# SwiGLU columns of both token tiles transposed in one batch and split in one instruction each

## The chip, the cores and the metric

One Trainium2 chip, one core of it. The metric is device time in microseconds of one execution of the whole program, a median over runs; lower is better.

## The reference

Two decoder layers over 256 tokens of width 1024. In each layer three attention mixers read one normalised input, an output projection adds to x, and a SwiGLU feed-forward (FFN) with 2816 inner columns follows. The FFN is the part that matters here:

```python
for l in range(DEPTH):              # DEPTH = 2
    ...
    x = x + mix @ w_out[l]
    h2 = rms_norm(x, ffn_norm_g[l])
    x = x + (jax.nn.silu(h2 @ w_gate[l]) * (h2 @ w_up[l])) @ w_down[l]
```

## The kernel before

All arithmetic is float32 through TensorE's fp32r type. Each product is made of three matmuls: every operand is split into a high part `h` (rounded by a copy to fp32r) and a low part `lo` (operand minus `h`), and `mm3` (L570 and after) issues high x high (L577), high x low weight (L578) and low x high weight (L579). Weights are split the same way, 1024 columns at a time, by a copy on ScalarE (L245, `wh<-raw`) and a subtraction on VectorE (L500, `wl<-raw,wh`).

The 256 tokens are two tiles of 128 (t = 0, 1; NT = 2). The FFN's 2816 columns are eleven chunks `fc` of 256, handled in the blocks (0), (1), (2,3), (4), (5,6), (7), (8,9), (10). A block of one chunk runs `alone`: for each tile, gate and up projections of 256 columns each into one PSUM bank. A block of two runs `strassen`: seven products, from which VectorE combines the gate and up sums of the four (chunk, tile) pairs in the order (second chunk, t=1), (second, t=0), (first, t=0), (first, t=1). For each pair a `glu_thread` then does: Silu of the gate half (L1184, ScalarE), times the up half (L1187 or L1190, VectorE) into a tile `p` of 256 columns; two 128x128 transposes on TensorE into a fresh PSUM bank (L595); a copy of their 256 columns to the high half of `f4` (L245 ScalarE, `qk<-bank`; `f4` lives in the buffer `qk`); and a subtraction to its low half (L1199, VectorE). Then the event `fev[fc][t]` lets `down` multiply `f4` by w_down into four PSUM banks, tile by tile. The down projection of a block follows the gate and up projections of the next block (inside `strassen` it stands after the fifth product).

No engine's order is written by hand. At build time a planner (`Timeline`) runs all these generators as threads. Each operation has an engine, a planned cost and a rank; the planner emits next the one that can start first by its clocks, and among equals the one of lower rank. The threads of SwiGLU have rank 10, the main thread of matmuls 50, the weight splits 60 once enough are ahead (5 before). The engines then run their queues strictly in the emitted order, so an operation that is later on the chip than in the plan holds up all that stands behind it on its engine. A `get` takes a free buffer: `PP` has seven tiles `p`, `BANK` eight PSUM banks, `HL` four split weights.

Of the kernel before, what the change touches and what calls it, by code (L numbers as in the profile page):

```python
# [9 lines left out]
F32 = mybir.dt.float32  # L10
# [5 lines left out]
P = 128  # L16
# [3 lines left out]
NT = S // P  # L20
# [3 lines left out]
NFC = DFF // FC  # L24
# [158 lines left out]
def hybrid_block(  # L183
# [18 lines left out]
    nc = tc.nc  # L202
    depth = w_in.shape[0]
    x_in = x_in[0]
    out = out[0]
# [16 lines left out]
    def slots(n, shape, tag):  # L222
        return Slots([tile_(shape, tag=tag) for _ in range(n)])


    def A(n, emit, sbuf=False, ap=0, bank=None):
        return ("op", [("ACT", n / 1.2 + (94 if sbuf else 51) + 93 * ap, emit)], bank)

    def V(n, emit, fast=False, ap=0, bank=None):
        return ("op", [("DVE", n / (1.92 if fast else 0.96) + 66 + 61 * ap, emit)], bank)  # L230
# [5 lines left out]
    def T(ns, emit):  # L236
        return ("op", [("PE", ns, emit)])

    def copy_op(dst, src, n, sbuf=False, scale=None, bank=None):

        ap = 0 if scale is None else 1

        def on_act():
            if scale is None:
                nc.scalar.activation(dst, src, AF.Copy)  # L245
            else:
                nc.scalar.activation(dst, src, AF.Copy, scale=scale)

        def on_dve():
            if scale is None:  # L250
                nc.vector.tensor_copy(dst, src)
            else:
                nc.vector.tensor_scalar_mul(dst, src, scale)

        a = A(n, on_act, sbuf, ap)[1]
        d = V(n, on_dve, sbuf, ap)[1]
        return ("op", a + d, bank)

    tl = Timeline()
# [3 lines left out]
    BANK = Slots(banks)  # L263
# [25 lines left out]
    PP = slots(7, [P, 3 * P], "p")  # L289
# [35 lines left out]
    def toks(t):  # L325
        return slice(t * P, (t + 1) * P)
# [7 lines left out]
    def quarters(b):  # L334
        return b.rearrange("p (k q) -> p k q", q=P)
# [229 lines left out]
    def drop(t, *key):  # L565
        ahead[0] -= 1
        HL.put(units[key]["hl"], t)
# [24 lines left out]
    def transposes(pairs):  # L592
        def emit():
            for o, i in pairs:
                nc.tensor.transpose(o, i, ident)  # L595

        return T(109 * len(pairs), emit)
# [576 lines left out]
        done.done(e)  # L1174


    def glu_thread(t, bank, src, full, f4_of, done):

        yield ("wait", full)
        ppt = yield ("get", PP)  # L1180
        ff = ppt[:, 0:FC]
        gu = bank if bank is not None else src[2]
        yield A(
            FC, lambda: nc.scalar.activation(ff, gu[:, 0:FC], AF.Silu), bank is None, bank=bank  # L1184
        )
        if bank is not None:
            e = yield V(FC, lambda: nc.vector.tensor_mul(ff, gu[:, FC : 2 * FC], ff), bank=bank)  # L1187
            BANK.put(bank, e)
        else:
            e = yield V(FC, lambda: nc.vector.tensor_mul(ff, gu[:, FC : 2 * FC], ff))  # L1190
            src[0].put(src[1], e)
        bank2 = yield ("get", BANK)
        b2 = quarters(bank2)
        e = yield transposes([(b2[:, k, :], ff[:, k * P : (k + 1) * P]) for k in range(2)])
        PP.put(ppt, e)
        f4 = yield from f4_of()
        h, lo = f4[:, 0:2, toks(t)], f4[:, 2:4, toks(t)]
        yield copy_op(h, b2[:, 0:2, :], 256, bank=bank2)
        e = yield V(256, lambda: nc.vector.tensor_sub(lo, b2[:, 0:2, :], h.bitcast(F32)), bank=bank2)  # L1199
        BANK.put(bank2, e)  # L1200
        done.done(e)

    def strassen_thread(at, ev, glu):
# [180 lines left out]
    def main():  # L1384
        for l in range(depth):
# [90 lines left out]
            full = [[Event(), Event()] for t in range(NT)]  # L1476
# [11 lines left out]
            for us, t in (((0, 1), 0), ((0,), 1), ((2, 3), 0), ((1,), 1), ((2, 3), 1)):  # L1488
# [6 lines left out]
                for u, k, kt, hf in order:  # L1495
                    wt = yield from weight(l, "out", OUT_ORDER[u][0], k=k)
                    yield ("wait", mix[mixed[u]][t])
                    e = yield mm3(
                        bk[t][hf], cur["mT"], kt, toks(t), wt, k, slice(512 * hf, 512 * hf + 512),
                        u == 0 and k == 0, u == 3 and k == 1,  # L1500
                    )
# [15 lines left out]
            def f4_of(fc):  # L1517
                def get():
                    yield ("wait", kept["over"])
                    if not f4s:  # L1520
                        f4s.append(tile_([P, 4, 4, S], F32R, tag="qk", own=False))
                    return f4s[0][:, fc % 4]

                return get

            fev = [[Event() for t in range(NT)] for fc in range(NFC)]
            x_ready[:] = [[Event(), Event()] for t in range(NT)]
            bk = full = None

            def down(fcs, t):  # L1530
                for fc in fcs:
                    key = (l, "down", fc)
                    yield ("wait", fev[fc][t])
                    f4 = f4s[0][:, fc % 4]
                    order = [(k, hf) for k in range(2) for hf in range(2)]
                    if fc == NFC - 1:
                        order.sort(key=lambda v: v[1])
                    for k, hf in order:
                        wt = yield from weight(*key, k=k)
                        e = yield mm3(  # L1540
                            bk[t][hf], (f4[:, 0:2], f4[:, 2:4]), k, toks(t), wt, k,
                            slice(512 * hf, 512 * hf + 512),
                            fc == 0 and k == 0, fc == NFC - 1 and k == 1,
                        )
                        if fc == NFC - 1 and k == 1:
                            full[t][hf].done(e)
                    if t == NT - 1:
                        drop(e, *key)
# [22 lines left out]
            def alone(fc):  # L1571
                for t in range(NT):
                    bank = yield ("get", BANK)
                    for u in (0, 4):
                        if fc == 0:
                            yield ("wait", h2_ready[t][u // 4])
                        for k in range(4):
                            wt = yield from weight(l, "gu", fc, u, k=k)
                            e = yield mm3(
                                bank, hT, u + k, toks(t), wt, k, slice(0, 512),  # L1580
                                u + k == 0, u + k == KT - 1,
                            )
                        if t == NT - 1:
                            drop(e, l, "gu", fc, u)
                    gfull = Event()
                    gfull.done(e)
                    tl.spawn(glu_thread(t, bank, None, gfull, f4_of(fc), fev[fc][t]), 10)

            def strassen(i, j, between):
                at = {}  # L1590
                ev = {k: Event() for k in "P1 P2 Q3 Q4 Q5 P6 P7".split()}

                def glu(t, n, src, when):
                    now = Event()
                    now.done(when)
                    fc = (i, j)[n]
                    tl.spawn(glu_thread(t, None, src, now, f4_of(fc), fev[fc][t]), 10)

                tl.spawn(strassen_thread(at, ev, glu), 8)
                lo8, hi8 = [tuple(h[:, ks] for h in hT) for ks in (slice(0, 4), slice(4, 8))]  # L1600
                s3, s1, s2, n4 = [(s_ready[o], kept, o) for o in range(4)]
                steps = [
                    ("P1", (lo8, 0), (l, "gu", i, 0)),
                    ("P7", s3, (l, "T3", i)),
                    ("Q5", s1, (l, "T1", i)),
                    ("P6", s2, (l, "T2", i)),
                    ("Q3", n4, (l, "gu", j, 4)),
                    None,
                    ("P2", (hi8, 0), (l, "gu", i, 4)),
                    ("Q4", (hi8, 1), (l, "T4", i)),  # L1610
                ]
                for step in steps:
                    if step is None:
                        yield from between
                        continue
                    name, a, key = step
                    at[name] = yield ("get", BANK)
                    if len(a) == 3:
                        yield ("wait", a[0])
                        aT, tok = kept["S"][a[2]], slice(0, P)  # L1620
                    else:
                        aT, tok = a[0], toks(a[1])
                    for k in range(4):
                        wt = yield from weight(*key, k=k)
                        e = yield mm3(
                            at[name], aT, k, tok, wt, k, slice(0, 512), k == 0, k == 3
                        )
                    drop(e, *key)
                    ev[name].done(e)
# [81 lines left out]
```

## Time and profile before

| | |
|---|---|
| median of 3 runs | 653.18 us (652.63 to 653.49) |
| profiled execution | 651.67 us, of which the span of the profile is 649.9 us |
| TensorE, VectorE, ScalarE, GpSimd busy | 636.6, 563.5, 401.2, 85.8 us |
| weight loads of TensorE busy | 521.6 us |
| granted clock of TensorE | 0.999 of full speed over the span |
| FFN of the first layer, of the second | some 147 to 330 us, some 465 to 647 us |

Busy time counts an instruction from its first to its last cycle, and neighbours overlap. So the time that an instruction takes from its engine is read from the distance between starts, not from its length. A matmul of 512 columns shows 0.39 us but starts 0.227 us after the one before it.

### The profile page before, as it was taken

To read this page: it belongs to the slowest core of one execution; us is meant where nothing else is said; L and a number is where in the kernel's file an instruction comes from. 1 tells how busy PE (TensorE), PEld (TensorE's weight loads), DVE (VectorE), ACT (ScalarE), POOL (GpSimd) and SP (SyncE) were. 2 spreads that over 40 slices of the span, in tenths; PEclk is the share of its full clock that TensorE was granted. 3 is DMA by queue.
4 is the path that set the end of the run, shared out by engine and by line. 5 is a ranking of instruction groups with operands and counts; after the bars stand their busy time and mean duration, and the time that the engine had idled before them with its cause. 6 is when DMAs were issued, how large, how long until landed. Compare 5 with 4: busy or idle time off the path is not lost.

```text
span 649.9 us, 8878 instructions
## 1 busy us (share of the span) xinstructions
PE 636.6 (98%) x3180; PEld 521.6 (80%) x3180; DVE 563.5 (87%) x948; ACT 401.2 (62%) x728; POOL 85.8 (13%) x115
## 2 busy tenths in 40 slices
PE   9999999999999999999999999999999999999997
PEld 8877887787787888878888788888777778888886
DVE  5889999666999999999487999985599899999971
ACT  6567587647656656556456675893677385575650
POOL 2513420200000000170020334300100000000000
PEclk9999999999999999999999999999999999999999
DMA  8972533608549458419747045352475475472631
GB/s 250 318 228 73 187 134 128 195 1 266 186 142 290 154 193 258 130 65 307 229 131 233 26 145 181 130 179 82 127 262 176 149 258 186 149 249 64 200 124 66
DMA packets 73777, 111.29 MB, mean 171 GB/s; under 512 B 2658, under 2 KB 54660, under 8 KB 73732
## 3 DMA queue, kind: packets, MB, share of 16 engines
q1 hardware_dynamic: 73700, 110.71, 52.8%
q8 instruction: 25, 0.41, 0.3%
q14 instruction: 20, 0.16, 0.1%
q10 hardware_dynamic: 32, 0.01, 0.0%
HBM read 109.66 MB, written 1.05 MB: 170 GB/s over the span
## 4 chain that ended last, share of the span: by engine, by line
PE 71%; DVE 18%; DMA 5%; ACT 2%; issue 2%; SPq 1%; POOL 0%; DVEq 0%; POOLq 0%; ACTq 0%
PE bank L577 21%; PE bank L579 20%; PE bank L578 20%; DVE wl L500 8%; PE bank L595 5%; DMA raw<-in_w_up_dram 3%; PE bank L996 2%; PE bank L1046 1%; DMA raw<-in_w_in_dram 1%; DVE raw L509 1%; DMA w<-in_diff_lambda_dram 1%; DVE qr L509 1%; DVE mL L509 1%; ACT wh L245 1%; DVE w L1211 1%
## 5 line engine op out<-in xcount | busy, mean ns | idle before, releaser
L245 ACT ACTIVATE wh<-raw 128x1024 fp32r<-128x1024 f32 (+3 forms) x207 | 210.8, 1040 | 98.9 <-PE bank L579 35.2
L500 DVE TENSOR_TENSOR wl<-raw,wh 128x1024 fp32r<-128x1024 f32 (+4 forms) x209 | 249.8, 1204 | 17.5 <-ACT wh L245 17.2
L577 PE MATMUL bank<-wh,hH 128*128 128x512 f32 (+3 forms) x488 | 191.6, 393 | 0.3 <-ACT hH L245 0.3
L578 PE MATMUL bank<-wl,hH 128*128 128x512 f32 (+3 forms) x488 | 186.1, 381 | 1.0 <-DVE wl L500 0.4
L579 PE MATMUL bank<-wh,hL 128*128 128x512 f32 (+3 forms) x488 | 185.2, 379 | 0.5 <-DVE hL L627 0.5
L578 PEld LDWEIGHTS bank<-wl,hH 128*128 128x128 f32 x488 | 92.0, 188 | 19.9 <-DVE wl L500 6.2
L577 PEld LDWEIGHTS bank<-wh,hH 128*128 128x128 f32 x488 | 91.9, 188 | 18.6 <-issue 3.6
L579 PEld LDWEIGHTS bank<-wh,hL 128*128 128x128 f32 x488 | 91.7, 188 | 17.3 <-DVE hL L627 0.8
L577 PE MATMUL bank<-wh,qk 128*128 128x512 f32 x176 | 69.5, 395 | 0.0
L579 PE MATMUL bank<-wh,qk 128*128 128x512 f32 x176 | 68.8, 391 | 0.3 <-DVE qk L1199 0.2
L578 PE MATMUL bank<-wl,qk 128*128 128x512 f32 x176 | 68.9, 391 | 0.2 <-DVE wl L500 0.2
L245 ACT ACTIVATE qk<-bank 128x256 fp32r<-128x256 f32 (+4 forms) x76 | 28.8, 405 | 37.7 <-PE bank L595 37.5
L579 PEld LDWEIGHTS bank<-wh,qk 128*128 128x128 f32 x176 | 33.1, 188 | 8.0 <-DVE qk L1199 1.1
L578 PEld LDWEIGHTS bank<-wl,qk 128*128 128x128 f32 x176 | 33.1, 188 | 7.6 <-DVE wl L500 1.0
L577 PEld LDWEIGHTS bank<-wh,qk 128*128 128x128 f32 x176 | 33.0, 188 | 6.6
L577 PE MATMUL bank<-wh,pv 128*128 128x512 f32 x96 | 37.5, 391 | 0.0
L578 PE MATMUL bank<-wl,pv 128*128 128x512 f32 x96 | 37.4, 389 | 0.0
L579 PE MATMUL bank<-wh,pv 128*128 128x512 f32 x96 | 37.4, 389 | 0.0
L977 ACT ACTIVATE p<-p,small 128x128 f32<-128x128 f32 (+1 forms) x64 | 28.4, 447 | 6.0 <-DVE small L966 6.0
L595 PE MATMUL bank<-ident,p 128*128 128x128 f32 x160 | 27.0, 275 | 4.2 <-DVE p L1187 2.6
L595 PEld LDWEIGHTS bank<-ident,p 128*128 128x128 f32 x160 | 20.0, 140 | 13.2 <-DVE p L1187 4.6
L716 DVE TENSOR_TENSOR x<-x,bank 128x512 f32<-128x512 f32 x16 | 11.0, 686 | 21.6 <-PE bank L579 21.6
(146 smaller groups left out, 925.6 us busy)
## 6 DMA issues: line engine op xcount, KB each, us to landing
raw<-in_w_in_dram SPq DMA_DIRECT2D x22, 1024.0 KB, 5.1
raw<-in_w_down_dram SPq DMA_DIRECT2D x22, 1024.0 KB, 5.0
raw<-in_w_gate_dram SPq DMA_DIRECT2D x32, 512.0 KB, 4.0
raw<-in_w_up_dram SPq DMA_DIRECT2D x32, 512.0 KB, 5.0
raw<-in_w_out_dram SPq DMA_DIRECT2D x8, 1024.0 KB, 4.9
raw<-in_w_in_dram SPq DMA_DIRECT2D x4, 768.0 KB, 4.9
tb<-in_w_gate_dram SPq DMA_DIRECT2D x4, 512.0 KB, 5.4
tb<-in_w_up_dram SPq DMA_DIRECT2D x4, 512.0 KB, 6.4
```

The costliest lines, as they stand in the source:

```text
L245: nc.scalar.activation(dst, src, AF.Copy)
L500: lambda: nc.vector.tensor_sub(lo[:, cs], raw[:, cs], h[:, cs].bitcast(F32)),
L509: return V(n, lambda: nc.vector.tensor_tensor(dst, a, b, op=op))
L577: nc.tensor.matmul(o, aH[:, kt, tok], wH[:, k, cols], start=start, stop=False)
L578: nc.tensor.matmul(o, aH[:, kt, tok], wL[:, k, cols], start=False, stop=False)
L579: nc.tensor.matmul(o, aL[:, kt, tok], wH[:, k, cols], start=False, stop=stop)
L595: nc.tensor.transpose(o, i, ident)
L716: e = yield V(512, lambda: nc.vector.tensor_add(xt[t][:, cs], xt[t][:, cs], bank))
L977: lambda: nc.scalar.activation(p[:, spans[t]], p[:, spans[t]], AF.Exp, bias=mn[:, t : t + 1], scale=-1.0, accum_out=se[t],),
L996: nc.tensor.matmul(two[e][:, t * P : t * P + n], qT[rows, pair, toks(t)], kT[rows, pair, :n], start=True, stop=True,)
L1046: nc.tensor.matmul(o, pT[:, toks(t)], v[0][:, cols], start=True, stop=t == 0)
L1211: 512, lambda: nc.vector.tensor_add(dst, at[name], other), bank=at[name]
```

## The change

The two transposes, the copy and the subtraction leave `glu_thread`. It now ends with the product in `p`, hands the tile over in `out`, and counts down an event `both[fc]`. A new `turn_thread` for each chunk waits until both tiles are there, takes one bank, makes four transposes into it (both tiles' columns side by side), returns both `p` tiles, copies 512 columns to the high half of `f4` in one instruction and subtracts 512 columns into the low half in one. `fev` now has one event a chunk, and `down` of either tile waits for it.

```diff
-    def glu_thread(t, bank, src, full, f4_of, done):
+    def glu_thread(bank, src, full, out, done):
...
-        bank2 = yield ("get", BANK)
-        b2 = quarters(bank2)
-        e = yield transposes([(b2[:, k, :], ff[:, k * P : (k + 1) * P]) for k in range(2)])
-        PP.put(ppt, e)
+        out.append(ppt)
+        done.done(e)
+
+    def turn_thread(ffs, both, f4_of, done):
+
+        yield ("wait", both)
+        bank = yield ("get", BANK)
+        b2 = quarters(bank)
+        e = yield transposes([
+            (b2[:, NT * k + t, :], ffs[t][0][:, k * P : (k + 1) * P])
+            for t in range(NT) for k in range(2)
+        ])
+        for t in range(NT):
+            PP.put(ffs[t][0], e)
         f4 = yield from f4_of()
-        h, lo = f4[:, 0:2, toks(t)], f4[:, 2:4, toks(t)]
-        yield copy_op(h, b2[:, 0:2, :], 256, bank=bank2)
-        e = yield V(256, lambda: nc.vector.tensor_sub(lo, b2[:, 0:2, :], h.bitcast(F32)), bank=bank2)
-        BANK.put(bank2, e)
+        h, lo = f4[:, 0:2, :], f4[:, 2:4, :]
+        src = bank.rearrange("p (k s) -> p k s", k=2)
+        yield copy_op(h, src, 512, bank=bank)
+        e = yield V(512, lambda: nc.vector.tensor_sub(lo, src, h.bitcast(F32)), bank=bank)
+        BANK.put(bank, e)
         done.done(e)
...
-            fev = [[Event() for t in range(NT)] for fc in range(NFC)]
+            fev = [Event() for fc in range(NFC)]
+            ffs = [[[] for t in range(NT)] for fc in range(NFC)]
+            both = [Event(NT) for fc in range(NFC)]
+            turned = set()
...
-                    yield ("wait", fev[fc][t])
+                    yield ("wait", fev[fc])
...
-                    tl.spawn(glu_thread(t, bank, None, gfull, f4_of(fc), fev[fc][t]), 10)
+                    tl.spawn(glu_thread(bank, None, gfull, ffs[fc][t], both[fc]), 10)
+                tl.spawn(turn_thread(ffs[fc], both[fc], f4_of(fc), fev[fc]), 10)
...
-                    tl.spawn(glu_thread(t, None, src, now, f4_of(fc), fev[fc][t]), 10)
+                    tl.spawn(glu_thread(None, src, now, ffs[fc][t], both[fc]), 10)
+                    if fc not in turned:
+                        turned.add(fc)
+                        tl.spawn(turn_thread(ffs[fc], both[fc], f4_of(fc), fev[fc]), 10)
```

## Rows read from the trace of the kernel before

**Rows 1.** The page: busy time by engine; the chain that ended last, by engine.

```profile
PE 636.6 (98%) x3180; PEld 521.6 (80%) x3180; DVE 563.5 (87%) x948; ACT 401.2 (62%) x728; POOL 85.8 (13%) x115
...
PE 71%; DVE 18%; DMA 5%; ACT 2%; issue 2%; SPq 1%; POOL 0%; DVEq 0%; POOLq 0%; ACTq 0%
```

**Rows 2.** Windows: stretch, its length, busy PE, PEld, DVE, ACT, POOL; clock, DMA.

```profile
150.00:153.00 3.00, 1.72 (x13) 1.31 (x12) 1.84 (x4) 2.48 (x4) 0.00 (x0) 1.00 1.09 349
...
189.00:207.00 18.00, 17.83 (x76) 13.53 (x75) 18.00 (x20) 8.02 (x10) 0.00 (x0) 1.00 0.66 200
```

**Rows 3.** Timeline of PE: a lone pair of transposes, then four together (start, length).

```profile
253.84 0.38 PE L595 MATMUL bank<-ident,p 128*128 128x128 f32 x2
...
254.53 0.39 PE L579 MATMUL bank<-wh,hL 128*128 128x512 f32 x1
...
256.38 0.60 PE L595 MATMUL bank<-ident,p 128*128 128x128 f32 x4
...
257.28 0.40 PE L579 MATMUL bank<-wh,hL 128*128 128x512 f32 x1
```

**Rows 4.** Timeline of DVE in the second layer, blocks (2,3) and (4).

```profile
526.11 0.75 DVE L1190 TENSOR_TENSOR p<-qr,p 128x256 f32<-128x256 f32 x2
...
533.29 0.42 DVE L1199 TENSOR_TENSOR qk<-bank,qk 128x256 fp32r<-128x256 f32 x1
...
535.89 0.42 DVE L1199 TENSOR_TENSOR qk<-bank,qk 128x256 fp32r<-128x256 f32 x1
536.22 1.22 DVE L500 TENSOR_TENSOR wl<-raw,wh 128x1024 fp32r<-128x1024 f32 x1
537.36 0.42 DVE L1187 TENSOR_TENSOR p<-bank,p 128x256 f32<-128x256 f32 x1
```

**Rows 5.** Groups by line: instructions | busy us, mean ns | idle before, releaser.

```profile
L245 ACT ACTIVATE w<-bank 128x512 f32<-128x512 f32 x6 | 3.6, 599 | 7.0 <-PE bank L579 7.0
...
L245 ACT ACTIVATE mH<-bank 128x256 fp32r<-128x256 f32 x8 | 3.0, 381 | 3.0 <-PE bank L595 2.9
```

**Rows 6.** Timeline of PE: transposes that come late, first layer.

```profile
174.83 0.39 PE L579 MATMUL bank<-wh,qk 128*128 128x512 f32 x1
175.35 0.44 PE L595 MATMUL bank<-ident,p 128*128 128x128 f32 x2
...
291.88 0.39 PE L579 MATMUL bank<-wh,qk 128*128 128x512 f32 x1
292.79 0.44 PE L595 MATMUL bank<-ident,p 128*128 128x128 f32 x2 [0.52 <-DVE p L1190]
...
294.46 0.38 PE L595 MATMUL bank<-ident,p 128*128 128x128 f32 x2
```

**Rows 7.** Waits of PE's weight loads, second layer from 472 us: total, times, longest.

```profile
PEld bank L595 <- DVE p L1187: 1.0, 2, 0.5
```

**Rows 8.** Timeline of PE and of DVE: the first down projection of layer one.

```profile
170.69 0.39 PE L578 MATMUL bank<-wl,qk 128*128 128x512 f32 x1
171.28 0.50 PE L579 MATMUL bank<-wh,qk 128*128 128x512 f32 x1 [0.20 <-DVE qk L1199]
```

```profile
170.81 0.42 DVE L1199 TENSOR_TENSOR qk<-bank,qk 128x256 fp32r<-128x256 f32 x1
```

**Rows 9.** Timeline of PE and of DVE: start of the FFN in layer one.

```profile
150.53 1.03 PE L595 MATMUL bank<-ident,w 128*128 128x128 f32 x8
152.84 0.44 PE L595 MATMUL bank<-ident,p 128*128 128x128 f32 x2 [1.28 <-DVE p L1187]
...
153.58 0.40 PE L579 MATMUL bank<-wh,hL 128*128 128x512 f32 x1
```

```profile
152.70 1.28 DVE L627 TENSOR_TENSOR hL<-qk,hH 128x512 fp32r<-128x512 f32 x2
```

**Rows 10.** Timeline of PE: down of block (2,3) begins, second layer.

```profile
533.49 0.39 PE L577 MATMUL bank<-wh,qk 128*128 128x512 f32 x1
...
533.94 0.39 PE L579 MATMUL bank<-wh,qk 128*128 128x512 f32 x1
```

## The prediction

> **What bounds the kernel now.** I read the page first: TensorE is busy 636.6 of 649.9 us and the chain that ended last is 71% TensorE and 18% VectorE [rows 1]. So a saving on ScalarE, GpSimd or the queues is worth nothing by itself, and one on VectorE only where TensorE stands waiting for it. The windows say where that is. In the stretch from 189 to 207 us of the first layer VectorE is busy 18.00 of 18.00 us and TensorE 17.83 [rows 2]: both are nearly full, TensorE misses a little, and what it waits for there is the split of weights. The reader should see that the two engines are close to a tie all through the FFN, with TensorE a little behind.
>
> Since matmuls overlap, I then went through TensorE's timeline by starts. Three matmuls of the down projection start at 533.49 to 533.94, so 0.45 us for two steps, 0.227 us each [rows 10]. Whatever exceeds 0.227 is a transpose or a wait. SwiGLU's transposes come late in a few places. At 175.35 the pair starts 0.52 us after the matmul before it, 0.29 more than a step; at 292.79 it is 0.91 us, 0.68 more [rows 6]. In the second layer TensorE's loads wait 1.0 us for the product L1187 in two places [rows 7]; about 0.2 us of each is a load's ordinary spacing (an estimate: at 292.79 the step is 0.227 of 0.91), so some 0.3 us each is lost. One more wait concerns the split: the first down projection of the first layer issues its third matmul 0.59 us after the second, 0.36 late, because the low half of f4 was made from 170.81 on [rows 8].
>
> **The batches on TensorE.** A lone pair: from its start at 253.84 to the second matmul after it, 254.53, is 0.69 us, less two steps (0.45) leaves 0.24. Four together: 256.38 to the third matmul, 257.28, is 0.90 us; that is the four transposes and two steps, so 0.45 [rows 3]. Two pairs cost 0.48, one four 0.45: 0.03 us a chunk at most, and with 22 chunks 0.6. Several pairs already adjoin (the four at 256.38 is two pairs in a row [rows 3]), and the starts are rounded to 0.01, so I take 0.2 us off; bounds 0 and 0.6.
>
> **VectorE and ScalarE.** Two 256-column operations back to back show 0.75 us, one 0.42, so an instruction takes 0.33 [rows 4]; two of 512 columns show 1.28 [rows 9], with some 0.68 for one alone, so 0.60. Two splits of 0.33 become one of 0.60: 0.06 us a chunk, 1.3 us over 22 chunks. ScalarE copies 256 columns in 0.381 us and 512 in 0.599 [rows 5], so it saves at most 0.16 a chunk, and with 8.02 busy of 18.00 [rows 2] I count that at nothing; its cover is TensorE's stream, and without it it would be 22 x 0.16 = 3.6 us. Of VectorE's 1.3 us I count only what lies ahead of a transpose that is late (next part). The stretch 189 to 207 has no split of f4 ahead of its waits that isn't followed by slack, so the rest is nothing; bounds 0 and 1.3 off.
>
> The Trainium skill, Perfetto Trace Analysis, section Optimizing Scalar/DVE Operations, puts the overhead of an instruction of VectorE on PSUM at about 125 ns and advises larger operations where the engine is saturated. By that figure the merged splits would save 22 x 0.125 = 2.75 us of VectorE, an estimate from the page, against 1.3 from the rows. The same section says that where the engine isn't saturated but causes bubbles elsewhere, smaller instructions may finish sooner, which speaks against the change. The trace decides between them by place: near saturation at 189 to 207, a bubble at 171.28.
>
> **The waits that go.** The transposes now wait for both tiles, so the first tile's pair can't stop TensorE any more; only the second tile's product can. The late pair at 175.35 is the first tile of chunk 1; before its partner TensorE shows no wait. So 0.29 goes, and one of the two like it in the second layer, 0.3. The pair at 292.79 is the first of chunk 9; the second is at 294.46 [rows 6], and would have been reached 0.68 sooner without the first stall. The product it needs ends about 0.25 before 294.46, so about 0.45 of the 0.68 returns: 0.2 gained. The other late place of the second layer is the second tile of chunk 4: its product at 537.36 is queued behind the first tile's split at 535.89 [rows 4]. That split now comes later, so the product moves up 0.33, and the 0.3 goes. Sum 1.1 us off; bounds 0 (each returns at the batch) and 1.8 (all of it and the partner's too).
>
> **The waits that come.** The low half of f4 for chunk 0 now takes 0.60 to 0.68 instead of 0.42 from 170.81 on, and the copy ahead of it 0.22 more. The copy has about as much slack; the split is late by 0.26. TensorE's matmul of 171.28 [rows 8] moves by that, in both layers: 0.5 us on. What is queued behind that split is a weight split, which gets it back when the second tile's split is gone. Next, the pair at 152.84 lies in a pause in which TensorE waits for the norm: eight transposes of the norm, a pause of 1.28, the pair, then the matmul of 153.58, which needs the low half made from 152.70 on [rows 9]. That pause hides the pair's 0.24. Moved out of it, the pair costs 0.24 in a full stream; the matmul behind it starts at most 0.14 sooner, as the norm's low half is ready at 153.38. So 0.1 on in each layer, 0.2.
>
> Everywhere else the batch has cover: down of a block comes after all gate and up projections of the next one, some 5 us or more after the last split. The bank is held once for 512 columns instead of twice for 256, the tiles p some microseconds longer, with at most four in use of seven. No DMA is moved.
>
> **Sum.** 0.2 + 1.1 off, 0.5 + 0.2 on: 0.6 us off. Against the profiled execution, 651.67, that is 651.1. That execution is 1.5 below the median of the runs; carried over to the median of 653.18 it is 652.6. What a measurement here can tell from no change is about 0.2%, 1.3 us, so the forecast is "the same". Its own range: at the top 0.7 on with nothing going, 653.9; at the bottom the 1.8 of waits off with half of the 0.7 coming, 651.7.
>
> **Rivals.**
>
> VectorE gives all of it back. The kernel's chain is 18% VectorE [rows 1], and a busy 18.00 of 18.00 means that time saved upstream may arrive. Then the whole 1.3 counts, with 0.6 for batches and 1.8 of waits, less 0.7: 3.0 off, 650.2. From 1.3 off on, 651.9, it counts as faster. For it: the tie of the two engines. Against: VectorE's splits come in bursts right after the transposes, where TensorE has work in hand.
>
> The split becomes the wait. Down of block (2,3) begins at 533.49 and needs the low half at 533.94 [rows 10]. Now that needs only the first tile's split; the second tile's starts at 533.29 [rows 4]. The merged one, started there, ends at 533.97: no slack left. If VectorE's queue puts it one weight operation later, TensorE loses 1.14 (536.22 to 537.36 [rows 4]), two later 2.3; block (2,3) of the first layer can add the same. It turns the sum at 0.6 and shows as slower at 1.9 us late in all. With two operations in one layer and one in the other, 3.4 late less 0.6 off and some of it made up by VectorE's slack, 655.0. For it: the rank of the splits lets the planner slip operations between. Against: the copy ends early enough to start the split before 533.29.
>
> The clock falls. Transposes now come four at a time. In the trace, eight in a row and then a pause of 1.28 us, and the clock stays 1.00, the full 2.4 GHz, in that window [rows 2, 9]. The price, if three matmuls after each of 22 batches ran at half the clock: 66 x 0.227 = 15 us (an estimate from the step), 668. The Trainium skill, TensorE: Matmul & The Clock Gate, Part 4, says that transposes don't count as activity for the clock the way matmuls do; the window above shows no trace of a cost.
>
> The change does nothing: waits only move from one tile to the other and 0.2 is all there is, 653.0. This lies inside the forecast's range and is counted with it.
>
> **Chances.** Forecast with the do-nothing case 0.46, of which 0.03 falls below 651.9 (faster) and none above 654.5; VectorE gives it back 0.31; the split becomes the wait 0.22; the clock 0.01. Faster 0.34, same 0.43, slower 0.23. The range takes in the forecast, somewhat more than half of the second case around its 650.2 (down to 649.8) and two thirds of the third around its 655.0 (up to 655.6); some 0.2 is left out.
>
> **What would show it.** Right: 88 transposes of SwiGLU in runs of four, 22 copies and 22 splits of 512 columns (about 0.60 and 0.68 us); no late transposes near 175 and 493; the first down matmul of each layer some 0.26 later against its neighbours; TensorE's busy share unchanged. Wrong: new waits of TensorE on the split of f4 at the start of down of block (2,3), or waits on the split of weights that shrink by more than 1 us. The planner's order changes with every planned cost, also far from the FFN's chunks; a shift of the weight splits in the second layer's mixers that costs or gives a microsecond is what my sum can't see.

## The result: 650.2 us, 0.5% faster, and not where the sum looked

| | before | after |
|---|---|---|
| median of 17 runs each, taken side by side | 653.70 us (651.07 to 658.03) | 650.22 us (648.09 to 653.93) |
| ratio, 95% interval | | 0.9947, 0.9929 to 0.9965 |
| profiled execution, its span | 651.67, 649.9 us | 648.09, 646.3 us |

The time fell inside the range given, near its lower edge, and almost on the number of the rival "VectorE gives all of it back" (650.2). The forecast itself, "the same", did not come: the sum said 0.6 us off, the medians differ by 3.5, and 0.5% is more than the 0.2% that counts as a difference. The range reaches down to 649.8 only because it takes in a part of that rival, and the rival's number is hit by another mechanism than the rival's, as the runs below show. So the hit is luck.

Some executions of every kernel show a mean granted clock of 0.993 to 0.997 instead of 0.999 to 1.000 and take 2 to 4 us longer; without them the changed kernel, run again as e5, gains 0.28% and not 0.44%.

The page of the changed kernel: busy time by engine, and the chain that ended last, by engine.

```profile
PE 632.8 (98%) x3180; PEld 522.0 (81%) x3180; DVE 561.2 (87%) x926; ACT 399.5 (62%) x706; POOL 85.6 (13%) x115
...
PE 80%; DVE 12%; DMA 4%; ACT 2%; issue 1%; SPq 0%; POOL 0%; DVEq 0%; ACTq 0%
```

Against [rows 1], TensorE runs the same 3180 matmuls in 3.8 us less, VectorE loses 22 instructions and 2.3 us, and VectorE's part of the chain falls from 18% to 12%. The windows that stand in [rows 2], of the kernel after (stretch, length, then busy PE, PEld, DVE, ACT, POOL, the clock, DMA):

```profile
150.00:153.00 3.00, 1.99 (x12) 1.23 (x10) 2.12 (x4) 2.31 (x4) 0.00 (x0) 1.00 1.09 348
189.00:207.00 18.00, 18.00 (x81) 14.70 (x80) 18.00 (x21) 9.06 (x11) 0.00 (x0) 1.00 0.71 234
```

From 189 to 207 us TensorE now starts 81 matmuls instead of 76 and VectorE does 21 operations instead of 20. Both still read full, so busy shares hardly show it; the counts do.

To place the 3.6 us between the spans, number the matmuls of 384 columns or more in both traces (2376 in each) and subtract the starts of equal numbers, after less before:

| start in the kernel before | 181.4 | 202.1 | 211.3 | 303.1 | 472.4 | 502.0 | 532.1 | 644.7 us |
|---|---|---|---|---|---|---|---|---|
| after less before | -0.20 | -0.52 | -1.93 | -2.50 | -2.23 | -2.03 | -3.73 | -3.59 us |

So 1.73 us come between 181.4 and 211.3 and 1.70 between 502.0 and 532.1: the same place in either layer, the end of the down projection of chunk 4 and the first half of block (5,6). Everything else together is 0.16. That rest is of this one pair of profiles: in e5's profile of the same changed kernel the two stretches give 1.88 and 1.84, but everything else costs 2.11 (the most of it a wait of 1.49 us on a weight split at 161.74, where before has 0.21), and the span is 1.6 us below before's. At that place the weight loads of TensorE waited for VectorE's weight split before, here in windows from 190 to 212 us and from 506 to 531 us (total, times, longest):

```profile
PEld bank L578 <- DVE wl L500: 2.3, 5, 0.5
...
PEld bank L578 <- DVE wl L500: 2.5, 5, 0.6
```

The same two windows after:

```profile
PEld bank L578 <- DVE wl L500: 0.3, 1, 0.3
...
PEld bank L578 <- DVE wl L500: 0.4, 1, 0.4
```

One of the five waits on TensorE's timeline before (start, length): the middle matmul comes 0.47 us after the one ahead of it, 0.25 more than a step, and the next comes 0.33 after it, 0.11 more.

```profile
203.66 0.39 PE L577 MATMUL bank<-wh,hH 128*128 128x512 f32 x1
204.13 0.50 PE L578 MATMUL bank<-wl,hH 128*128 128x512 f32 x1
204.46 0.39 PE L579 MATMUL bank<-wh,hL 128*128 128x512 f32 x1
```

The cause stands on VectorE some microseconds earlier. Its timeline before:

```profile
184.15 2.35 DVE L500 TENSOR_TENSOR wl<-mH,wh 128x1024 fp32r<-128x1024 f32 x2
187.96 1.23 DVE L509 TENSOR_TENSOR mH<-mL,tb 128x1024 f32<-128x1024 f32 x1 [1.46 <-DMA tb<-in_w_up_dram]
189.10 1.22 DVE L500 TENSOR_TENSOR wl<-raw,wh 128x1024 fp32r<-128x1024 f32 x1
```

And after:

```profile
183.80 2.35 DVE L500 TENSOR_TENSOR wl<-mH,wh 128x1024 fp32r<-128x1024 f32 x2
186.07 1.22 DVE L500 TENSOR_TENSOR wl<-raw,wh 128x1024 fp32r<-128x1024 f32 x1
187.99 1.23 DVE L509 TENSOR_TENSOR mH<-mL,tb 128x1024 f32<-128x1024 f32 x1 [0.69 <-DMA tb<-in_w_up_dram]
```

L509 is the first sum of weights of Strassen's block (5,6), and it needs a piece of w_up that comes late: it starts at 187.96 and at 187.99, in each trace 0.12 us after the load has landed. Before, VectorE stood idle for 1.46 us in front of it with ready weight splits queued behind. After, the planner has put one split ahead of the sum. VectorE is then one split further from there on, and all of the five waits but one of 0.3 us go. In the second layer the idle stretch falls from 1.67 to 0.87 us. There the profile names no load as its end, but the load of w_up lands at 505.83 before and at 504.05 after, 0.18 and 0.17 us ahead of the sum.

### The profile page after: what moved, and what is told of

Its sections match the earlier page's. It is cut to its first block, busy times and chain, and to the rows that moved or that the text cites. A ratio compares the mean times of both kernels' runs of the same rounds, so it can differ in the third digit from the quotient of the medians.

```text
span 646.3 us, 8829 instructions
## 1 busy us (share of the span) xinstructions
PE 632.8 (98%) x3180; PEld 522.0 (81%) x3180; DVE 561.2 (87%) x926; ACT 399.5 (62%) x706; POOL 85.6 (13%) x115
## 4 chain that ended last, share of the span: by engine, by line
PE 80%; DVE 12%; DMA 4%; ACT 2%; issue 1%; SPq 0%; POOL 0%; DVEq 0%; ACTq 0%
PE bank L577 24%; PE bank L579 23%; PE bank L578 23%; DVE wl L500 5%; PE bank L595 5%; PE bank L996 2%; DMA raw<-in_w_up_dram 2%; PE bank L1046 1%; DMA raw<-in_w_in_dram 1%; PE bank L913 1%; DMA x<-in_x_dram 1%; PE bank L1048 1%; ACT wh L245 1%; DVE tb L509 1%; DVE pv L660 1%
## 5 line engine op out<-in xcount | busy, mean ns | idle before, releaser
L245 ACT ACTIVATE qk<-bank 128x512 fp32r<-128x512 f32 (+4 forms) x54 | 26.1, 502 | 35.0 <-PE bank L595 34.4
L577 PE MATMUL bank<-wh,mH 128*128 128x512 f32 x64 | 25.9, 405 | 0.0
L1350 POOL TENSOR_TENSOR tb<-gqk,ropes 128x192 f32<-128x192 f32 x8 | 9.0, 1131 | 123.8 <-DVE wl L500 122.8
```

The costliest lines, as they stand in the source:

```text
L577: nc.tensor.matmul(o, aH[:, kt, tok], wH[:, k, cols], start=start, stop=False)
L1350: yield G(550, lambda: nc.gpsimd.tensor_tensor(cur["rc"][:, t, js, :], gl[:, s], cc, op=OP.mult))
```

## The experiments

The theory, "order": which of the two stands first, the split or the late sum, decides the time. The rivals: "VectorE's time" (the saved 1.3 us arrive, the prediction's rival), and "batches" (each saved instruction and wait counts where it stands). In the runs below only VectorE's order, or only the batch, is changed as far as the planner allows.

**One part alone: the order without the batch.** The kernel before, with the moment from which the planner lets the first sum of block (5,6) be emitted put back by 1.0 us (e1) or 0.2 us (e4). A split then goes ahead; the chip's own waits are as they were.

```diff
-            yield ("wait", b22["raw"])
+            yield ("wait", later(b22["raw"], 1000.0 if (i, j) == (5, 6) else 0.0))
```

> The kernel before, with one change to the planner's dates: the first sum of block (5,6) (VectorE L509, mH<-mL,tb), which waits for a late load of w_up, is planned 1.0 us later, in both layers. VectorE's order changes in that one place of each layer: a split of weights (and one combination of the products) now stands ahead of the sum. TensorE's, ScalarE's and the DMA order stay as they were; no batching. Theory 'order': the gain of the change comes from that split filling VectorE's pause before the late load, so this kernel is some 2 to 3.4 us faster than before (ratio 0.995 to 0.997), and TensorE's waits for weight splits at 192 to 208 us and 510 to 526 us go. Theory 'VectorE's time' (22 merged splits give it back): nothing merged, ratio 1.000. Theory 'batches' (fewer late transposes): 1.000.

> As the first of these kernels, but the sum is planned only 0.2 us later. The split goes ahead of the sum here too, and the planner's later choices follow the shift (TensorE's transposes and products of block (2,3) stand in another order). Theory 'order': 2 to 3.4 us faster than before, and it shows that 0.2 us of planned time decide. The other theories: 1.000, give or take what the other choices cost.

e1 was a miss: 0.9999 (0.9976 to 1.0022). Its timeline of VectorE says why. Two operations moved ahead, as expected, but the second, a combination of Strassen's products (L1211), waits for TensorE, so that the sum starts at 189.42, 1.46 later than before:

```profile
186.90 1.22 DVE L500 TENSOR_TENSOR wl<-raw,wh 128x1024 fp32r<-128x1024 f32 x1
188.81 0.69 DVE L1211 TENSOR_TENSOR w<-bank,w 128x512 f32<-128x512 f32 x1 [0.70 <-PE bank L579]
189.42 1.21 DVE L509 TENSOR_TENSOR mH<-mL,tb 128x1024 f32<-128x1024 f32 x1
```

Three of five waits remained in either layer (1.3 us each). With 0.2 us, e4, the split alone goes ahead, and the sum behind it doesn't wait at all:

```profile
185.34 1.22 DVE L500 TENSOR_TENSOR wl<-raw,wh 128x1024 fp32r<-128x1024 f32 x1
186.48 1.21 DVE L509 TENSOR_TENSOR mH<-mL,tb 128x1024 f32<-128x1024 f32 x1
```

None of the ten waits is left, and the kernel takes 0.9962 (0.9938 to 0.9986) of before without a single batch.

**The batch without the order.** The changed kernel, with that sum planned 0.8 us earlier, so that it stands ahead of the split again (e2).

```diff
-            u["raw"].done(t + 2000.0)
+            u["raw"].done(t + 2000.0); u["soon"].done(t + 2000.0 - 800.0)
...
-            yield ("wait", b12["raw"])
-            yield ("wait", b22["raw"])
+            yield ("wait", b12["soon" if (i, j) == (5, 6) else "raw"])
+            yield ("wait", b22["soon" if (i, j) == (5, 6) else "raw"])
```

> The changed kernel, with the same sum planned 0.8 us earlier, so that it stands ahead of the split of weights again, as before the change. Batches and merged copies and splits stay. Theory 'order': nearly all the gain but the 0.6 us of the batches is lost, ratio to the kernel before 0.998 to 1.000, with TensorE's waits for splits at 192 to 208 us back. Theory 'VectorE's time' or 'batches': it stays near 0.995.

1.0027 (1.0000 to 1.0054): with all 22 batches in place the gain is gone. VectorE's timeline shows the idle stretch in front of the sum again:

```profile
187.16 1.23 DVE L509 TENSOR_TENSOR mH<-mL,tb 128x1024 f32<-128x1024 f32 x1 [1.49 <-DMA tb<-in_w_up_dram]
```

and the waits of its weight loads from 190 to 212 us are those of the kernel before:

```profile
PEld bank L578 <- DVE wl L500: 2.2, 5, 0.5
```

Part of the loss in e2's profile is another one, a batch of transposes 1.33 us late at 622.23, told of with e8.

**The batch without the merged instructions.** The changed kernel in its own order on every engine, but each copy and split of 512 columns issued as two of 256 (e3).

```diff
-        yield copy_op(h, src, 512, bank=bank)
-        e = yield V(512, lambda: nc.vector.tensor_sub(lo, src, h.bitcast(F32)), bank=bank)
+        yield A(512, lambda: [nc.scalar.activation(h[:, :, c], src[:, :, c], AF.Copy) for c in cs], bank=bank)
+        e = yield V(512, lambda: [nc.vector.tensor_sub(lo[:, :, c], src[:, :, c], h[:, :, c].bitcast(F32)) for c in cs], bank=bank)
```

> The changed kernel with the same order on every engine, but each merged copy and each merged split issued as two instructions of 256 columns (22 more on ScalarE, 22 more on VectorE). Theory 'VectorE's time': the 1.3 us of VectorE are taken back and the gain with it, ratio to before 0.997 or above. Theory 'order': the order holds, so the ratio stays at 0.994 to 0.996; at most 0.5 us are lost, or some gained where the first tile's low half is ready sooner.

0.9970 (0.9946 to 0.9994), span 645.9 against 646.3 us. The interval would allow either theory; the trace doesn't. With the 22 instructions back, the waits of 190 to 212 and 506 to 531 us are 0.3 and 0.2 us, as in the changed kernel. What the merge saves is small. VectorE's timeline of e3, where the pair takes 0.67 us to the next start:

```profile
170.02 0.74 DVE L1210 TENSOR_TENSOR qk<-bank,qk 128x256 fp32r<-128x256 f32 x2
170.69 1.21 DVE L500 TENSOR_TENSOR wl<-raw,wh 128x1024 fp32r<-128x1024 f32 x1
```

and of the changed kernel, where the merged one takes 0.60:

```profile
170.59 0.68 DVE L1210 TENSOR_TENSOR qk<-bank,qk 128x512 fp32r<-128x512 f32 x1
171.19 1.22 DVE L500 TENSOR_TENSOR wl<-raw,wh 128x1024 fp32r<-128x1024 f32 x1
```

**More splits ahead, and chunk 0 mended.** Beside the changed kernel itself (e5): two splits ahead of the sum (e6, the late loads planned 3500 instead of 2000 ns after their issue); chunk 0 alone copied and split per tile behind its batch, so that down's first tile can start on the first half (e7); and e7 with the sum planned 0.4 us later (e8).

```diff
-            fev = [Event() for fc in range(NFC)]
+            fev = [[Event(), Event()] if fc == 0 else [Event()] * NT for fc in range(NFC)]
...
-                    yield ("wait", fev[fc])
+                    yield ("wait", fev[fc][t])
```

> The changed kernel once more, unaltered, as a yardstick for the three runs beside it on this chip. Every theory expects 0.993 to 0.9965 of before (the interval already measured); a ratio above 0.998 would say that the 3.5 us between the kernels are partly a matter of the occasion.

> The changed kernel, with the late expert-up loads planned 1.5 us later, so that two weight splits, not one, stand ahead of the first sum of block (5,6) in VectorE's order. Theory 'order' (one split ahead is enough to take the idle stretch in front of the sum, and it is that stretch, 1.46 us before and 0.69 after, that the gain comes from): the second split fills the 0.69 us that are left, at most another 0.7 us per layer on VectorE, and none of TensorE's five waits on splits comes back; 0.993 to 0.998 of before, equal to the changed kernel within 0.3%. Rival 'the sum is then late': the sum's product is needed some 2 us later and TensorE waits for it, 0.6 us or more per layer, so 0.996 to 1.001. Theory 'batches alone' (VectorE's saved time, whatever the order): no difference to the changed kernel.

> The changed kernel, with chunk 0 alone copied and split per token tile (its transposes still a batch of four), so that the down product's first tile starts on the first half. The waits of 0.50 us at 171.33 and 0.52 us at 487.39 go, 0.2 to 0.4 us per layer. But the VectorE order that the planner lays down changes with it: both sums of block (5,6) stand ahead of the splits again, as in the kernel before. Theory 'order': the idle stretch in front of the sum and the waits on splits come back, which takes 2.5 us or more, so 0.997 to 1.002 of before although a predicted wait was removed. Theory 'batches alone': the gain stays and grows by 0.4 to 0.8 us, so 0.992 to 0.9955.

> The run before it with the sum of block (5,6) planned 0.4 us later, so that a weight split stands ahead of it again, as in the changed kernel. Theory 'order': the waits on splits stay away and chunk 0's wait is shorter too, so 0.9925 to 0.996 of before, equal to the changed kernel or up to 0.8 us faster. Theory 'batches alone': the same as the run before it. It differs from that run in VectorE's order alone, so the two tell the theories apart.

e5: 0.9956 (0.9932 to 0.9980), so the difference holds on another occasion. e6: 0.9944 (0.9917 to 0.9971), no wait on a split left, and the sum, though it starts only at 191.53, isn't missed by TensorE. e7: 0.9992 (0.9965 to 1.0019), as "order" said, yet not only for its reason. e8: 0.9988 (0.9961 to 1.0015), a miss for "order": all ten waits on splits are gone, and still nothing is gained. TensorE's timeline of e8 shows what was overlooked:

```profile
174.97 0.50 PE L579 MATMUL bank<-wh,qk 128*128 128x512 f32 x1 [1.04 <-DVE qk L1211]
```

and VectorE's the operations ahead of that split:

```profile
172.23 1.22 DVE L509 TENSOR_TENSOR raw<-mL,raw 128x1024 f32<-128x1024 f32 x1
173.36 1.22 DVE L500 TENSOR_TENSOR wl<-raw,wh 128x1024 fp32r<-128x1024 f32 x1
174.50 0.42 DVE L1211 TENSOR_TENSOR qk<-bank,qk 128x256 fp32r<-128x256 f32 x1
```

The second half's split, now an operation of its own, is queued behind a sum and a weight split; the matmul that needs it is 1.2 us late, in both layers, in e7 and in e8. So the first half's wait was mended (0.50 to 0.16 us) and a larger one made. e8's profile also shows a batch 1.23 us late at 619.76. Its product is ready to be made but queued behind a split whose load of w_down is late; VectorE has the same order there in e7, and no such wait. The profiles of e2 and e10 have the like at this place, the others not: the same trap as at 188 us, in some executions only.

**Which batch moves the order.** The change made for some chunks only: for chunk 0 (e9), for all but chunk 0 (e10), for chunk 3 (e11).

```diff
+    BATCH = {(0, 0), (1, 0)}
...
-                tl.spawn(turn_thread(ffs[fc], both[fc], f4_of(fc), fev[fc]), 10)
+                if (l, fc) in BATCH:
+                    tl.spawn(turn_thread(ffs[fc], both[fc], f4_of(fc), fev[fc][0]), 10)
```

> The kernel before, with the change made for chunk 0 of each layer alone: 2 of the 22 batches. Chunk 0 is where the prediction saw a loss (0.5 us over both layers) and no gain. But this one batch is enough to make the planner put a weight split ahead of the first sum of block (5,6) in both layers. Theory 'order': the stretch from the third matmul of block (5,6) on gains 1.2 us or more per layer, as in the changed kernel, and the time is 0.9935 to 0.997 of before. Theory 'batches' (saved instructions and waits, each where it stands): two batches save 0.1 us and the chunk's later low half costs 0.5, so 1.000 to 1.0015.

> The changed kernel, with chunk 0 of each layer left as in the kernel before: 20 of the 22 batches. The first sum of block (5,6) stands ahead of the split again, as before. Theory 'order': the five waits on weight splits are back in most part, the stretch gains 0 to 0.8 us per layer instead of 1.4 to 1.9, and the time is 0.9975 to 1.0005 of before. Theory 'batches': ten elevenths of the gain stay and chunk 0's 0.5 us isn't paid, so 0.993 to 0.996.

> The kernel before, with the change made for chunk 3 of each layer alone. The planner then puts a split ahead of a sum in block (8,9) only; block (5,6) keeps its order. Theory 'order': what such a flip is worth depends on whether a late load stands at the head of VectorE's queue there, and in the kernel before block (8,9) shows no stop of a microsecond, so 0 to 0.6 us per layer: 0.998 to 1.001. Theory 'batches': two batches, 0.1 us, 0.9995 to 1.0005. The two overlap here; the run shows what a flip without an idle stretch is worth, by the stretch's own starts.

Two batches of 22 bring the gain: e9 takes 0.9957 (0.9931 to 0.9982). Twenty of 22 bring none: e10 takes 1.0012 (0.9986 to 1.0038), a little above what was expected. VectorE's timeline of e10:

```profile
185.72 2.35 DVE L500 TENSOR_TENSOR wl<-mH,wh 128x1024 fp32r<-128x1024 f32 x2
189.64 1.23 DVE L509 TENSOR_TENSOR mH<-mL,tb 128x1024 f32<-128x1024 f32 x1 [1.57 <-DMA tb<-in_w_up_dram]
```

and of e9:

```profile
186.48 1.22 DVE L500 TENSOR_TENSOR wl<-raw,wh 128x1024 fp32r<-128x1024 f32 x1
188.33 1.23 DVE L509 TENSOR_TENSOR mH<-mL,tb 128x1024 f32<-128x1024 f32 x1 [0.64 <-DMA tb<-in_w_up_dram]
```

As before and after: 1.57 us idle without a split ahead, 0.64 with one. The second layer shows that for the waits on splits the split done ahead counts, and not the idle time. In e9 the sum stands idle there for 1.47 us even behind the split (1.24 in e10, without one), because its load lands only 6.5 us after its issue, at 505.23:

```profile
505.41 1.23 DVE L509 TENSOR_TENSOR mH<-mL,tb 128x1024 f32<-128x1024 f32 x1 [1.47 <-issue]
```

Four of the five waits on splits stay away all the same.

e11, a flip in block (8,9) alone, is 0.9984 (0.9962 to 1.0007): nothing that can be told from the time. By the starts, the first layer gains 0.54 us between 211.3 and 303.1, and the second loses 1.66 between 546.3 and 580.0, where 0 to 0.6 gained was expected. Why it loses was not found.

All profiles side by side. "Waits" are those on the split in the two windows, us and times; "moved" is the change of the start difference from before's 181.4 to 211.3 us and from 502.0 to 532.1 us; "full clock" is the ratio of the means of those executions, of either kernel, whose granted clock was 0.998 or more.

| kernel | ahead of the sum | ratio | full clock | waits | moved, us |
|---|---|---|---|---|---|
| before | nothing | 1 | 1 | 2.3, 5; 2.5, 5 | |
| changed | split | 0.9947 | not on record | 0.3, 1; 0.4, 1 | -1.73; -1.70 |
| e5, changed again | split | 0.9956 | 0.9972 | none; 0.3, 1 | -1.88; -1.84 |
| e3, unmerged | split | 0.9970 | 0.9972 | 0.3, 1; 0.2, 1 | -1.46; -1.93 |
| e6, two splits | splits | 0.9944 | 0.9965 | none; none | -1.76; -1.99 |
| e4, no batch | split | 0.9962 | 0.9969 | none; none | -1.84; -1.78 |
| e9, chunk 0 only | split | 0.9957 | 0.9955 | 0.3, 1; 0.4, 1 | -1.59; -0.71 |
| e8, chunk 0 per tile | split | 0.9988 | 0.9990 | none; none | -1.80; -2.04 |
| e1, no batch | split and L1211 | 0.9999 | 1.0000 | 1.3, 3; 1.3, 3 | -0.72; -0.89 |
| e7, chunk 0 per tile | nothing | 0.9992 | 1.0003 | 1.0, 2; 1.6, 4 | -0.86; -0.76 |
| e2, changed | nothing | 1.0027 | 1.0022 | 2.2, 5; 2.5, 5 | -0.18; -0.10 |
| e10, all but chunk 0 | nothing | 1.0012 | 1.0007 | 2.7, 5; 2.3, 5 | +0.33; -0.24 |
| e11, chunk 3 only | nothing | 0.9984 | 0.9997 | 2.1, 5; 1.8, 4 | -0.29; -0.39 |

The last column sorts by the second, whatever is batched; e1 and e7 lie in between. (In e9's second layer a matmul at 518.80 is 0.66 us late, waiting for VectorE to release a bank; the operation that releases it, L1237, starts 1.19 us later than its like in the changed kernel, as does the late sum ahead of it, 505.41 against 504.22.) Nor does any ratio speak against it but e8's, whose loss lies elsewhere: at the full clock the other kernels with splits alone ahead have 0.9955 to 0.9972, those with nothing ahead and e1 0.9997 to 1.0022. So the swap is worth some 2 to 3 us of an execution. In most of these profiles the two stretches gain more, 3.4 to 3.8 us; where the rest goes was not found.

## Why the prediction came out as it did

**What bounds the kernel** was read rightly: TensorE a little behind VectorE, waiting for weight splits at 189 to 207 us.

**The step that failed** is the last of the part on VectorE: "The stretch 189 to 207 has no split of f4 ahead of its waits that isn't followed by slack, so the rest is nothing." The slack meant is the idle 1.46 us in front of the late sum. It does swallow time saved ahead of it as long as the order stays; e2 and e10 show that. But idle time in front of a late operation, with ready work behind, is a price paid in the kernel before, and it goes when the planner swaps the two. The prediction named the planner's order as what its sum couldn't see, and named waits on weight splits shrinking by more than 1 us as the sign of being wrong. They shrank by 4.1 us in the two windows, and 3.4 of the 3.6 us between the two profiled spans came with them.

**The rival "VectorE gives all of it back"** has the right number by the wrong way, that is by luck. Time saved on VectorE doesn't arrive: e3 spends it again and keeps the gain, e2 keeps it and loses the gain.

**Batches on TensorE**, 0.2 us off: from 546.3 to 616.4 us of before, with batches that only change places, the start difference goes from -3.45 to -3.49, and in e5's profile from -1.27 to -1.51. Small, as said, and within the bounds. (The matmul at 254.53 is the third behind the lone pair, not the second; the one at 257.28 is the third behind the four, so 0.24 and 0.45 are measured alike.)

**VectorE's 0.06 us a chunk**: 0.67 less 0.60, so 0.07. The estimate from the Trainium skill, Perfetto Trace Analysis, section Optimizing Scalar/DVE Operations, of 0.125 us an instruction is too much here. That section's other sentence, on bubbles that smaller instructions may shorten, is borne out by e8 for the first half at 171 us (0.50 us late merged, 0.16 split again), but the second half then came 1.2 us late.

**The waits that come.** TensorE's timeline after, at the places of [rows 8] and [rows 6]:

```profile
170.60 0.39 PE L578 MATMUL bank<-wl,qk 128*128 128x512 f32 x1
171.33 0.50 PE L579 MATMUL bank<-wh,qk 128*128 128x512 f32 x1 [0.34 <-DVE qk L1210]
...
174.86 0.39 PE L579 MATMUL bank<-wh,qk 128*128 128x512 f32 x1
175.09 0.74 PE L595 MATMUL bank<-ident,p 128*128 128x128 f32 x4
...
291.34 0.39 PE L579 MATMUL bank<-wh,qk 128*128 128x512 f32 x1
291.92 0.66 PE L595 MATMUL bank<-ident,p 128*128 128x128 f32 x4 [0.20 <-DVE p L1190]
```

The first down projection's third matmul is 0.50 late instead of 0.36, in the second layer 0.52 instead of 0.22: 0.44 on in all, 0.5 predicted. The pair that left the norm's pause did so: the matmul there waits for the copy instead, and the start difference is -0.29 at 149.2 us and -0.33 at 158.6, so nothing was lost there; at 166.4 it is -0.09, the 0.24 of a pair, paid in the stream as predicted.

**The waits that go.** The late pair at 175.35 and its twin are gone, 0.29 and 0.27, with 0.09 and 0.10 left inside the batches; so is the second layer's of chunk 4 (0.26). At 291.92 the batch is 0.36 late, 0.68 before: 0.33 gained where 0.2 was said. (e11, without that batch, gains 0.74 at the same place, so that the batch is the cause there is not shown.) These terms were right in place and near in size. That they add up, with the waits that come, to the 0.6 us of the sum is not shown: in this pair of profiles 0.16 us off are left, but 0.29 off stand already at 149.2 us, ahead of the first batch, and in e5's profile the same rest is 2.11 us on.

**"The split becomes the wait"** came in a small way, at the place named: the third matmul of down of block (2,3) in the second layer, at 530.40, is 0.19 late and the next 0.11. In e7 and e8 the same mechanism at chunk 0 costs 1.2 us a layer. **The clock** stayed at 1.00 in both windows above, and its mean over the span is 1.000: 22 runs of four transposes cost nothing there. Among the profiles only e6's shows a fall inside the kernel: the granted clock is 0.50, the 1.2 GHz level, for 6.8 us from 121.8 us on, in the mixers of the first layer, ahead of the first batch. TensorE had run transposes and short matmuls there, with pauses of 0.76 and 0.69 us; e5's profile has the same pauses and no fall. The start difference of e6 goes from -0.74 to +2.50 us over it, so one such fall costs about as much as the change gains.

**What stays open.** The batch of chunk 0 is what moves the planner, and it makes its first difference on VectorE some 17 us before the sum. Which part of it (the saved time on the planner's clock, or the products that come earlier in the order) tips the choice was not tried. Nor is it shown whether the change has a part in how often the clock falls.

## What to carry to other kernels

In a kernel whose queues are laid down by a planner, look for operations that stand idle on a late load while ready work is queued behind them, and count that idle time as something that any edit ahead may win or lose. The terms of a small edit can each be right to a few tenths and their sum still miss the result, because the edit moves such a choice far away; changing only the order, then only the edit, tells the two apart. When a part of a batch is split off again, see what its second half gets queued behind.

## Not expected of the hardware

A matmul that has waited delays the next one as well: 0.33 us instead of 0.23 between 204.13 and 204.46, the same 0.11 behind every one of the ten waits. So a wait on a split costs TensorE 0.11 us more than its length, and the ten waits of 0.07 to 0.35 us on the timeline, 2.1 us together, cost 3.2.
